# Two RG-LRU tiles moved among the RWKV chunks, their sums moved behind the latents' products, four weight differences on another engine, and a fourth residual buffer

## The chip, the cores and the metric

One core of a Trainium2 chip runs the program. Its engines work from queues of their own and wait for one another by semaphores: TensorE (PE, matmuls; PEld is its loading of the stationary operand), VectorE (DVE), ScalarE (ACT), GpSimd (POOL) and SyncE (SP), which here issues nearly all DMAs. The metric is the device time of one execution in microseconds, lower is better. One execution was also taken by the profiler; its page and its trace are what the text quotes.

## The reference

Two layers of a hybrid block over 512 tokens of width 1024. Each layer norms the residual stream, projects it, feeds three mixers, and adds their gated outputs, projected, to the stream:

```python
for l in range(DEPTH):
    xn = rms_norm(h, ln_g[l])
    proj = xn @ w_in[l]
    u_a, z_a, u_b, z_b, q_lat, kv_lat, k_rope, z_c = jnp.split(proj, pts, axis=-1)
    y_a = rwkv7_mix(u_a, ...)                      # delta rule, 8 heads of 64
    y_b = rms_norm(rglru_mix(u_b, ...), ...)       # gated linear recurrence over 512 channels
    y_c = rms_norm(mla_mix(q_lat, kv_lat, ...))    # latent attention, 8 heads
    y = jnp.concatenate([y_a * silu(z_a), y_b * silu(z_b), y_c * silu(z_c)], axis=-1)
    h = h + y @ w_out[l]
return rms_norm(h, final_g)
```

The second mixer is the one that the change moves:

```python
xc = conv_b + sum(up[:, j:j + T] * conv_w[j] for j in range(4))
gate_r = sigmoid(einsum('bthi,hij->bthj', xb, ga_w) + ga_b)   # gate_i likewise with gx
log_a = -8 * gate_r * softplus(-lam)
a = exp(log_a)
bx = sqrt(-expm1(2 * log_a)) * (gate_i * xc)
h_t = a_t * h_{t-1} + bx_t
```

## The kernel before

All products of a weight with an activation are made of three fp32r matmuls (`mm3`, L231): each operand is split into a high part and the difference to it (low part), and high-high, high-low and low-high are added in PSUM. For weights this is `weights` (L217): SP loads 128x512 into `wr` (three buffers), ACT copies it to `wH`, and POOL or DVE subtracts to make `wL` (four buffers each). Which of the two subtracts is counted: every `wmod`-th call of `weights` goes to DVE, all others to POOL.

A layer is a list of steps, written out as strings (L61 to L63) that `run` goes through. A letter names the step and a digit its tile. `ORD1` is the preparation of the RWKV mixer, `ORD2` its inverses together with gates and projections, `ORD3` the rest:

- `H0` to `H7` (`chunk`, L840) are the eight chunks of 64 tokens of the delta rule. Each needs the state of the one before: matmuls L848, an addition on DVE (L851), matmuls L858, additions on DVE (L862, L863), and every second chunk its output (L876, L882, L884 to L886).
- `A0` to `A3` (`lru_a`, L671) are the four tiles of 128 channels of the RG-LRU: a projection (24 matmuls, two weight loads), the convolution (three L680 on DVE), two gates (L686 on PE, sigmoids on ACT), a product on POOL (L690) and a tanh.
- `B0` and `B1` (`lru_b`, L696) finish tiles 0 and 1, or 2 and 3: exponentials, squares on POOL (L701), L703 and L704 on DVE, square roots, L709 on POOL, the scan (L711), its squares (L717 on ACT) added into `stb` on POOL (L718), and the gating (L719).
- `R0` (`b_sums`, L938) makes the mean square of each token by eight matmuls over `stb` (L378) and a reciprocal root on DVE (`rsb`). `Y0` (`b_split`, L941) splits the four outputs for the product with `w_out`.
- `N0` (`group_norm`, L890) norms the RWKV outputs (small operations L198 to L203 and four L894 on DVE).
- `t0` to `t7` (`lat_products`, L900) are the products of the latents: per step one weight tile of 416 columns (L906) and twelve matmuls, three for each of four token tiles. They use all four `acc` buffers of PSUM. `T0` copies them out, `T1` norms them.
- `g0` to `g3` are the gates 25 to 28 of the attention: a projection into an `acc` buffer, a copy on ACT (L141), a sigmoid, a product on POOL.

Behind `ORD3`, `Q1` (L65) interleaves key, value and query products with `out_parts` (L412, the letter `o`), which adds the RG-LRU's part to the residual stream: for each half of the columns it takes four residual tiles `hp` (L419, tag with three buffers) and four `acc` buffers, multiplies four weight tiles, scales by `rsb` and adds (L427), and writes the tiles to DRAM (L429). `a` steps (`ya_step`, L971) transpose the normed RWKV outputs on PE (L978).

At the start, before the layers, each of four token tiles of `x` is squared on ACT, its reciprocal root is found by small operations on DVE (L245 to L255), it is scaled (L297 on DVE), transposed on PE (L302) and split (L305). The first two projections run among these tiles.

The strings set priorities, not the order itself: when the program is built a planner goes through the instructions of each engine, takes the one with the lowest place in the text among those that its table of costs says are ready, and so fixes the order of every queue. Each engine then runs its queue strictly in that order. So a projection that stands late in the text runs early where PE would otherwise wait, and an instruction whose operands come later than planned holds up all that is queued behind it. The activation function tables (`act`, L133) are used strictly in the order of the text.

Of the kernel before, what the change touches and what calls it, by code (L numbers as in the profile page):

```python
# [12 lines left out]
ALU = mybir.AluOpType  # L13
# [34 lines left out]
def body(ctx, tc, x, wc, wl, wo, w2a2, gagx, wuq, wukv, vec, ln_g, fin_g, cst, out, depth=DEPTH):  # L48
    nc = tc.nc
    V, A, G = nc.vector, nc.scalar, nc.gpsimd  # L50
# [9 lines left out]
    BN = (2, 2, 0, 0)  # L60
    ORD1 = "M0 L0 L1 C0 M1 C1 P0 L2 O0 M2 U1 O1 C2 U2 P1 L3 M3 C3 U0 P2 O2"  # L61
    ORD2 = "G0 U3 G1 P3 G2 Z0 Z1 O3 G3 X0 f4 V0 V1 Z2 Q0 Q1 f0 V2 V3 f1 Q2 Q3 J0 f2 J1 K0 f3 W0 K1 W1 f5 W2 W3"
    ORD3 = "B0 H0 H1 H2 H3 A3 H4 H5 H6 H7 N0 A2 B1 g0 g1 R0 t0 t6 t1 t2 t4 Y0 t5 t3 t7 T0 g2 g3 T1"  # L63
    LO = "0ig12uw3yvcm"
    Q1 = "aoooottttaaaooookvvqvkqvkqkqqqqq"  # L65
    WA, WB, WC, WD = 1000, 2, 2, 5
# [1 line left out]
    def tl(tag, shape, dt=F32, bufs=1):  # L68
        cnt[0] += 1
        return SB.tile(list(shape), dt, tag=tag, name=f"{tag}_{cnt[0]}", bufs=bufs)  # L70
# [4 lines left out]
    def c2(shape=(128, 512), dt=F32):  # L75
        return tl("c2", shape, dt, bufs=7)
# [33 lines left out]
    def acc(shape=(128, 512)):  # L110
        cnt[0] += 1
        return PS.tile(list(shape), F32, tag="acc", name=f"acc_{cnt[0]}", bufs=4)

    def spill():
        cnt[0] += 1
        return DR.tile([128, 512], F32, name=f"dr_{cnt[0]}")
# [23 lines left out]
    def copy(out, in_, **kw):  # L140
        i = A.activation(out=out, in_=in_, func=AF.Copy, **kw)  # L141
        return getattr(i, "ins", i)
# [63 lines left out]
    def f(ap):  # L206
        return ap.bitcast(F32)
# [6 lines left out]
    wn = [0]  # L214
    wmod = [4]

    def weights(src, n=512, raw=None):  # L217

        if raw is None:
            raw = tl("wr", [128, n], F32, bufs=3)  # L220
            nc.sync.dma_start(out=raw, in_=src)
        H = tl("wH", [128, n], F32R, bufs=4)
        L = tl("wL", [128, n], F32R, bufs=4)
        wn[0] += 1
        i = copy(H, raw)
        if behind:
            tc.add_manual_dep(i, behind.pop(0).name, NOSYNC, reason="issue order")
        (V if wn[0] % wmod[0] == 0 else G).tensor_tensor(out=L, in0=raw, in1=f(H), op=ALU.subtract)  # L228
        return H, L

    def mm3(o, a, b, start, stop):  # L231
        PE.matmul(o, a[0], b[0], start=start, stop=False)  # L232
        PE.matmul(o, a[0], b[1], start=False, stop=False)  # L233
        PE.matmul(o, a[1], b[0], start=False, stop=stop)  # L234
# [85 lines left out]
    def one_layer(l):  # L320
# [9 lines left out]
        def proj(j, halves=False):  # L330

            if halves:
                o = acc()
                W = [weights(wc[l, j, :, 4 * hf:4 * hf + 4, :].rearrange("p k c -> p (k c)"), raw=raws.pop((j, hf), None)) for hf in range(2)]
                for th in range(2):
                    t = slice(th * 256, (th + 1) * 256)
                    for k in range(8):
                        s = slice((k % 4) * 128, (k % 4 + 1) * 128)
                        w = W[k // 4]
                        mm3(o[:, t], (w[0][:, s], w[1][:, s]), (xH[:, k, t], xL[:, k, t]), k == 0, k == 7)  # L340
                return o
            o, parts = proj_parts(j)
            for part in parts:
                part()
            return o

        def proj_parts(j):
            o = acc()

            def part(hf):  # L350
                H, L = weights(wc[l, j, :, 4 * hf:4 * hf + 4, :].rearrange("p k c -> p (k c)"))
                for k in range(4):
                    s = slice(k * 128, (k + 1) * 128)
                    kk = 4 * hf + k
                    mm3(o, (H[:, s], L[:, s]), xk(kk), kk == 0, kk == 7)

            return o, [lambda: part(0), lambda: part(1)]
# [33 lines left out]
        def out_steps(m, y):  # L391

            W, os = {}, {}

            def step(n, tt, k):
                if tt == 0 and k == 0:
                    W[n] = [weights(wo[l, m, n, :, i, :]) for i in range(4)]
                if k == 0:
                    os[n, tt] = tl("hp", [128, 512], bufs=3), acc()
                    nc.sync.dma_start(out=os[n, tt][0], in_=hsrc[tt, n])  # L400
                hp, o = os[n, tt]
                c = slice(tt * 128, (tt + 1) * 128)
                mm3(o, (y[k][:, 0, c], y[k][:, 1, c]), W[n][k], k == 0, k == 3)
                if k == 3:
                    V.tensor_tensor(out=hp, in0=o, in1=hp, op=ALU.add)
                    hd = spill()
                    nc.sync.dma_start(out=hd, in_=hp)
                    hsrc[tt, n] = hd

            return [lambda n=n, tt=tt, k=k: step(n, tt, k) for n in range(2) for tt in range(4) for k in range(4)]  # L410

        def out_parts(m, y, rs):  # L412

            os = {}

            def part(n, k):
                if k == 0:
                    for tt in range(4):
                        os[tt] = tl("hp", [128, 512], bufs=3), acc()  # L419
                        nc.sync.dma_start(out=os[tt][0], in_=hsrc[tt, n])  # L420
                W = weights(wo[l, m, n, :, k, :])
                for tt in range(4):
                    c = slice(tt * 128, (tt + 1) * 128)
                    mm3(os[tt][1], (y[k][:, 0, c], y[k][:, 1, c]), W, k == 0, k == 3)
                for tt in range(4) if k == 3 else ():
                    hp, o = os[tt]
                    V.scalar_tensor_tensor(out=hp, in0=o, scalar=rs[:, 2 * tt:2 * tt + 1], in1=hp, op0=ALU.mult, op1=ALU.add)  # L427
                    hd = spill()
                    nc.sync.dma_start(out=hd, in_=hp)  # L429
                    hsrc[tt, n] = hd  # L430

            return [lambda n=n, k=k: part(n, k) for n in range(2) for k in range(4)]
# [212 lines left out]
        def run(order):  # L645
            for s in order.split():
                steps[s[0]](int(s[1]))
# [128 lines left out]
        R0 = {}  # L776
# [169 lines left out]
        run(ORD2)  # L946
        run(ORD3)
        rsb = misc["rsb"]
# [276 lines left out]
```

## Time and profile before

| what | value |
|---|---|
| time, median of 3 runs | 868.64 us (867.18 to 869.16) |
| the profiled execution: time, span | 868.69 us, 866.8 us |
| mean granted TensorE clock | 0.978 |
| RWKV chunks (first L858 to the latents' products) | 204.4 to 255.1 us and 627.8 to 678.3 us |
| latents' products (to gate 27) | 255.1 to 284.6 us and 678.3 to 707.7 us |
| bytes over DMA | 91.08 MB, mean 105 GB/s |

The first of each pair is layer 0, the second layer 1. In rows of the trace the columns are the start, the time taken, engine, line and operation, output and input, the number of instructions merged in the row, and in brackets the idle time before it with what ended it. In rows of waits they are who waited, for whom, total, times, longest. In windows they are the length, the busy time of each engine with the number of instructions, the granted clock (1.00 is full speed), the share of the DMA engines and GB/s. In groups they are line, engine, operation, shapes and count, then busy time and mean ns of one, then the idle time before them.

### The profile page before, as it was taken

The page shows a single profiled execution, that of the slowest core. Times are in us where ns is not written, and L with a number is a line of the kernel's source. Part 1 is how long each engine was busy: PE and PEld are TensorE (multiplying, and loading weights), DVE is VectorE, ACT ScalarE, POOL GpSimd, SP SyncE. Part 2 cuts the span into 40 slices and gives each one's busy share as a digit, 9 for nine tenths or more (in the row PEclk, how much of TensorE's full clock was granted, in tenths as well). Part 3 has the DMA queues.
Part 4 walks back from the last instruction along what each step waited for, and adds up shares of the span by engine and source line. Part 5 has one row for each costly group of instructions (what it writes and reads, how often), then busy time and mean ns, then how long its engine had stood idle before and what let it go on. Part 6 is the DMA issues. An engine that isn't in the chain of part 4 may idle for free.

```text
span 866.8 us, 15212 instructions
## 1 busy us (share of the span) xinstructions
PE 801.0 (92%) x5696; PEld 624.3 (72%) x5696; DVE 574.6 (66%) x1169; ACT 506.2 (58%) x990; POOL 332.3 (38%) x303
## 2 busy tenths in 40 slices
PE   3999999999896999999989999999998699999995
PEld 2877888877676867566778788888766597765674
DVE  5678776924887485875474866694367856777736
ACT  5667875656544635574367677745572644455635
POOL 2355557513325431011444556574151544210123
PEclk9999999999998989999999999999999989999998
DMA  6322233310112465122743233232101134741354
GB/s 218 115 70 69 72 110 134 116 51 26 31 43 81 136 206 186 56 87 96 250 139 98 74 98 106 89 109 92 39 14 51 45 107 137 232 130 50 109 170 159
DMA packets 49755, 91.08 MB, mean 105 GB/s; under 512 B 5520, under 2 KB 8336, under 8 KB 49680
## 3 DMA queue, kind: packets, MB, share of 16 engines
q1 hardware_dynamic: 49104, 89.05, 31.8%
q8 instruction: 45, 0.74, 0.3%
q10 hardware_dynamic: 576, 1.05, 0.3%
q14 instruction: 30, 0.25, 0.1%
HBM read 73.30 MB, written 16.78 MB: 104 GB/s over the span
## 4 chain that ended last, share of the span: by engine, by line
PE 43%; DVE 10%; ACT 5%; DMA 3%; issue 2%; POOL 2%; SPq 0%; ACTq 0%; DVEq 0%; POOLq 0%
PE acc L232 9%; PE acc L233 9%; PE acc L234 9%; PE acc L1057 4%; PE ck L1083 3%; PE ps L1075 2%; DMA hp<-dr 1%; ACT g L138 1%; DMA wr<-in_wo_dram 1%; ACT UV L141 1%; DVE c L460 1%; PE ps L686 1%; PE ps L610 1%; ACT wH L141 1%; DVE wL L228 1%
## 5 line engine op out<-in xcount | busy, mean ns | idle before, releaser
L228 POOL TENSOR_TENSOR wL<-wr,wH 128x512 fp32r<-128x512 f32 (+1 forms) x130 | 175.6, 1355 | 308.7 <-ACT wH L141 301.8
L141 ACT ACTIVATE wH<-wr 128x512 fp32r<-128x512 f32 (+1 forms) x192 | 119.0, 622 | 139.7 <-PE acc L233 73.3
L232 PE MATMUL acc<-xH,wH 128*128 128x512 f32 (+1 forms) x496 | 191.4, 387 | 0.0
L233 PE MATMUL acc<-xL,wH 128*128 128x512 f32 (+1 forms) x496 | 189.8, 383 | 0.4 <-DVE xL L305 0.3
L234 PE MATMUL acc<-xH,wL 128*128 128x512 f32 (+1 forms) x496 | 189.4, 382 | 0.0
L232 PEld LDWEIGHTS acc<-xH,wH 128*128 128x128 f32 x496 | 94.0, 190 | 19.2 <-issue 1.6
L233 PEld LDWEIGHTS acc<-xL,wH 128*128 128x128 f32 x496 | 94.3, 190 | 17.6 <-DVE xL L305 1.2
L234 PEld LDWEIGHTS acc<-xH,wL 128*128 128x128 f32 x496 | 94.2, 190 | 17.1
L228 DVE TENSOR_TENSOR wL<-wr,wH 128x512 fp32r<-128x512 f32 (+1 forms) x62 | 47.3, 765 | 69.0 <-ACT wH L141 68.4
L232 PE MATMUL acc<-wH,c 128*128 128x512 f32 x192 | 83.7, 436 | 2.5 <-DVE hp L427 1.2
L233 PE MATMUL acc<-wL,c 128*128 128x512 f32 x192 | 77.6, 404 | 1.1 <-DVE wL L228 1.1
L234 PE MATMUL acc<-wH,c 128*128 128x512 f32 x192 | 77.3, 403 | 0.0
L141 ACT ACTIVATE UV<-ps 64x512 f32<-64x512 f32 (+4 forms) x112 | 52.4, 494 | 32.0 <-PE ps L1075 22.5
L232 PEld LDWEIGHTS acc<-wH,c 128*128 128x128 f32 x192 | 37.2, 194 | 12.8 <-ACT c L141 2.9
L138 ACT ACTIVATE c<-acc,sm 128x128 f32<-128x128 f32 (+3 forms) x64 | 33.5, 526 | 19.4 <-DVE sm L1059 19.1
L233 PEld LDWEIGHTS acc<-wL,c 128*128 128x128 f32 x192 | 37.1, 193 | 9.5 <-DVE wL L228 1.5
L1057 PE MATMUL acc<-am,am 128*128 128x128 f32 (+3 forms) x128 | 42.3, 447 | 0.9 <-ACT c L138 0.8
L234 PEld LDWEIGHTS acc<-wH,c 128*128 128x128 f32 x192 | 36.9, 192 | 8.6 <-issue 0.5
L138 ACT ACTIVATE g<-g 128x512 f32<-128x512 f32 (+1 forms) x58 | 36.1, 626 | 8.4 <-DVE g L704 6.5
L136 ACT ACT_TABLE_LOAD x31 | 39.8, 1283 | 1.3 <-PEq L1213 0.7
L141 ACT ACTIVATE c<-g 128x512 fp32r<-128x512 f32 (+1 forms) x40 | 25.0, 630 | 21.5 <-DVE g L980 16.1
L368 POOL TENSOR_TENSOR g<-g,g 128x512 f32<-128x512 f32 x24 | 32.6, 1360 | 10.4 <-ACT g L138 10.4
(221 smaller groups left out, 1604.4 us busy)
## 6 DMA issues: line engine op xcount, KB each, us to landing
wr<-in_wc_dram SPq DMA_DIRECT2D x116, 256.0 KB, 2.7
wr<-in_wo_dram SPq DMA_DIRECT2D x48, 256.0 KB, 3.4
hp<-dr SPq DMA_DIRECT2D x40, 256.0 KB, 3.2
dr<-hp SPq DMA_DIRECT2D x32, 256.0 KB, 2.8
dr<-g SPq DMA_DIRECT2D x16, 256.0 KB, 2.6
g<-dr SPq DMA_DIRECT2D x16, 256.0 KB, 2.9
wr<-in_wl_dram SPq DMA_DIRECT2D x16, 208.0 KB, 2.5
c<-in_x_dram SPq DMA_DIRECT2D x8, 256.0 KB, 6.5
```

Source lines behind the costliest of these rows:

```text
L136: chained(A.preload_act_table_set(SETS[st]))
L138: chained(A.activation(out=out, in_=in_, func=func, **kw))
L141: i = A.activation(out=out, in_=in_, func=AF.Copy, **kw)
L228: (V if wn[0] % wmod[0] == 0 else G).tensor_tensor(out=L, in0=raw, in1=f(H), op=ALU.subtract)
L232: PE.matmul(o, a[0], b[0], start=start, stop=False)
L233: PE.matmul(o, a[0], b[1], start=False, stop=False)
L234: PE.matmul(o, a[1], b[0], start=False, stop=stop)
L368: G.tensor_tensor(out=z, in0=z, in1=s, op=ALU.mult)
L460: V.scalar_tensor_tensor(out=hv, in0=o, scalar=rs[:, 2 * tt:2 * tt + 1], in1=hp, op0=ALU.mult, op1=ALU.add)
L1057: PE.matmul(o[:, 0:n], qT[:, hd, qt * 128:n], K2[:, p, e, 0:n], start=True, stop=True)
L1075: PE.transpose(o[:, (qt - kt) * 128:(qt - kt + 1) * 128], Pm[p][e, qt][:, kt * 128:(kt + 1) * 128], ident)
L1083: i = PE.matmul(ot[e * 64:(e + 1) * 64, k2 * 128:T], Vt[:, k2, 2 * p + e, :], PT[:, 2 * (k2 % 2) + e, 0:(4 - k2) * 128], start=(k2 == 0), ...
```

## The change

```diff
-    ORD3 = "B0 H0 H1 H2 H3 A3 H4 H5 H6 H7 N0 A2 B1 g0 g1 R0 t0 t6 t1 t2 t4 Y0 t5 t3 t7 T0 g2 g3 T1"
+    ORD3 = "B0 H0 H1 A2 H2 H3 A3 H4 H5 H6 H7 B1 N0 g0 g1 t0 t6 t1 t2 t4 t5 t3 t7 T0 R0 Y0 g2 g3 T1"
...
-        (V if wn[0] % wmod[0] == 0 else G).tensor_tensor(out=L, in0=raw, in1=f(H), op=ALU.subtract)
+
+        (V if wn[0] % wmod[0] == 0 or wn[0] <= 4 else G).tensor_tensor(out=L, in0=raw, in1=f(H), op=ALU.subtract)
...
-                        os[tt] = tl("hp", [128, 512], bufs=3), acc()
+                        os[tt] = (tl("hp", [128, 512], bufs=3) if tt < 3 else c2()), acc()
```

`A2` goes from behind the group norm to behind the second chunk. `B1` goes ahead of the group norm. `R0` and `Y0` go behind the latents' products and their copies. The first four calls of `weights` in the program (the projections 12 and 0 of layer 0) subtract on DVE. In `out_parts` the fourth residual tile of each half comes from the pool `c2` (seven buffers, L76), which the chunks' outputs and later the attention's probabilities also use. No operation is added or left out.

## The prediction

> **What bounds the kernel now.** First the page's head and busy table, then the waits of PE stage by stage, then the stretch with the largest wait in windows and in order of time. Both layers show it alike; the rows are layer 1's where none is named.
>
> ```profile
> span 866.8 us, 15212 instructions
> PE 801.0 (92%) x5696; PEld 624.3 (72%) x5696; DVE 574.6 (66%) x1169; ACT 506.2 (58%) x990; POOL 332.3 (38%) x303
> ...
> 255.12:284.56 29.44, 22.77 (x110) 21.54 (x109) 22.09 (x35) 15.23 (x25) 16.51 (x12) 0.88 0.22 68
> 678.27:707.74 29.47, 22.81 (x110) 21.58 (x108) 22.17 (x35) 15.20 (x25) 16.54 (x12) 0.88 0.22 69
> ...
> PE ck L378 <- POOL sqn L718: 5.2, 1, 5.2
> PE acc L233 <- DVE wL L228: 1.5, 1, 1.5
> ```
>
> PE is busy for 801.0 of 866.8 us, so 65.8 us of it are idle, and what ends late on PE sets the time. The two windows run from the first product of the latents to the first of gate 27, in layer 0 and in layer 1 (columns: length, then PE, PEld, DVE, ACT, POOL busy, the granted clock, DMA). PE stands idle for 29.47 - 22.81 = 6.66 us of each, in two waits: 5.2 us of the token sums (L378) for POOL, 1.5 us of a product for a weight difference from DVE.
>
> ```profile
> 678.27 0.35 PE L232 MATMUL acc<-wH,xH 128*128 128x416 f32 x1
> 679.95 0.35 PE L232 MATMUL acc<-wH,xH 128*128 128x416 f32 x1
> 686.82 0.35 PE L234 MATMUL acc<-wH,xL 128*128 128x416 f32 x1
> 678.77 4.19 DVE L894 TENSOR_TENSOR c<-c,vr 128x512 f32<-128x512 f32 x4
> 682.88 1.28 DVE L703 SCALAR_TENSOR_TENSOR g<-g,g 128x512 f32<-128x512 f32 x2
> 685.30 2.53 POOL L709 TENSOR_TENSOR g<-g,g 128x512 f32<-128x512 f32 x2 [3.50 <-ACT g L138]
> 689.65 3.11 POOL L718 TENSOR_TENSOR sqn<-sqn,g 128x512 f32<-128x512 f32 x2 [1.82 <-ACT g L717]
> 691.11 0.58 ACT L141 ACTIVATE g<-acc 128x512 f32<-128x512 f32 x1
> 692.81 1.86 PE L378 MATMUL ck<-ones,sqn 128*128 128x2 f32 x8 [5.21 <-POOL sqn L718]
> 692.00:694.00 2.00, 1.19 (x6) 1.19 (x6) 1.31 (x1) 0.81 (x2) 2.00 (x2) 0.50 0.00 0
> 696.00:698.00 2.00, 2.00 (x7) 1.90 (x7) 1.93 (x5) 1.55 (x3) 1.08 (x1) 0.50 0.00 0
> 698.00:700.00 2.00, 2.00 (x11) 1.96 (x10) 1.90 (x6) 0.55 (x1) 1.33 (x1) 0.87 0.42 107
> ```
>
> The rows in order of time show why. Step B1 (L699 to L720 for tiles 2 and 3) stands behind the group norm: its L703 starts at 682.88, when L894 has let DVE go. Then follow square root, L709, scan, square and L718, one engine waiting for the next, and L378 stands in PE's queue ahead of the remaining products. A second cause hides under it. From 678.27 to 686.82 PE runs 36 products: four weight tiles for three token tiles each (4 x 3 x 3). The fourth token tile needs the accumulator of gate 26, which ACT copies out only at 691.11, behind the squares of B1. So it is not enough to move the sums: B1 must be early as well. After the wait the granted clock is 0.50 from 692.81 to 698 (the first and the last of three windows stand here) and 0.87 to 700, which loses half of 5.19 us and 0.13 of 2, or 2.9 us. The stall's whole price is **6.66 + 2.9 = 9.6 us a layer**.
>
> **The change, part by part.** *Sums behind the products, B1 ahead of the group norm.* R0 now comes after T0. Its eight matmuls and the vector work on `rsb` remain; the first use is L427, behind 48 matmuls of gates 27 and 28 and 48 of the first output half, 18 us even at the 0.187 us below, so R0 is hidden. Behind L378 on PE now stand gate 27's products, and they would wait only if B1 were late by the whole run of the latents' products. Y0 issues the same splits later, with the same cover. What is late next is the products' supply: from the first to the tenth start is 1.68 us, 0.187 each, so a tile of 12 asks for its weights every 2.24 us. The 1.5 us wait for DVE came behind L894, L703 and L704; with B1 gone, L894 is still there. I keep 1.0 us of it (bounds 0 and 1.5). The stage gives **8.6 us a layer**.
>
> *A2 among the chunks.* Nothing is added: the same 24 matmuls, two weight loads, three L680, gates and activations, ahead of H2 instead of behind N0. The planner already fills the gaps between chunk steps with the projections of A3, A2 and gates 25 and 26, so on PE and in SP's queue A2 and A3 only change places. What moves is behind the projection: A2's three L680 now outrank H2, A3's gates come before H4, and B1 with its two table changes and six POOL operations falls into H4 to H7, where DVE's queue also holds the additions L851, L862 and L863 that the next chunk's matmuls wait for.
>
> ```profile
> 627.80:655.90 28.10, 25.11 (x345) 18.16 (x344) 19.64 (x36) 16.21 (x26) 11.60 (x10) 1.00 0.13 39
> 655.90:674.30 18.40, 17.64 (x279) 12.60 (x278) 11.74 (x25) 6.47 (x13) 3.13 (x3) 1.00 0.09 25
> L680 DVE SCALAR_TENSOR_TENSOR g<-g,vecs,g 128x512 f32<-128x512 f32 x4 | 3.0, 746 | 0.0
> L719 DVE SCALAR_TENSOR_TENSOR g<-g,vecs,g 128x512 f32<-128x512 f32 x2 | 2.5, 1262 | 0.0
> L711 DVE TENSOR_TENSOR_SCAN g<-g,g 128x512 f32<-128x512 f32 x2 | 2.4, 1224 | 0.6 <-POOL g L709 0.6
> L703 DVE SCALAR_TENSOR_TENSOR g<-g,g 128x512 f32<-128x512 f32 x2 | 1.4, 692 | 1.8 <-POOL g L701 0.9 <-POOL g L675 0.9
> L709 POOL TENSOR_TENSOR g<-g,g 128x512 f32<-128x512 f32 x2 | 2.6, 1280 | 4.2 <-ACT g L138 4.2
> L863 DVE TENSOR_TENSOR S<-S,PC x12: 404/416/428, 218.3 to 669.8; 128x256 f32<-128x256 f32 x12
> ```
>
> The first window is B0 and the early chunks, the second the late ones. B0 is the same work for tiles 0 and 1, and beside it PE idles 28.10 - 25.11 = 3.0 us; without it 18.40 - 17.64 = 0.8. If B1 does to the late chunks what B0 does to the early ones, that is 2.2 us a layer. B1's DVE part is 2.5 + 2.4 + 1.4 and some 0.8 for L704, about 7.1 us, and DVE is free for 18.40 - 11.74 = 6.7 us of that window, plus the 3.0 us of four L680 that leave it; projections still stand ready. Bounds are a gain of 0.8, the idle that there is to lose, and all of it in the chunks' chain: 7.1 us and six L680 of 0.75, or 11.6. I take **1.5 us** a layer, near the row of B0, and the remaining products as cover; without that cover it is the 2.2.
>
> *First four differences on DVE.*
>
> ```profile
> 11.88 0.16 DVE L254 SCALAR_TENSOR_TENSOR sm<-sm,sm 128x1 f32<-128x1 f32 x1
> 12.50 2.49 POOL L228 TENSOR_TENSOR wL<-wr,wH 128x512 fp32r<-128x512 f32 x2 [11.04 <-ACT wH L141]
> 12.55 1.23 DVE L255 SCALAR_TENSOR_TENSOR sm<-sm,sm 128x1 f32<-128x1 f32 x1
> 13.82 2.38 DVE L297 SCALAR_TENSOR_TENSOR g<-c,sm,c 128x512 f32<-128x512 f32 x2
> 18.99 1.26 DVE L253 TENSOR_TENSOR sm<-sm 128x1 f32<-128x1 f32 x1
> 20.29 1.20 DVE L254 SCALAR_TENSOR_TENSOR sm<-sm,sm 128x1 f32<-128x1 f32 x1
> 21.71 1.41 DVE L297 SCALAR_TENSOR_TENSOR g<-c,sm,c 128x512 f32<-128x512 f32 x2
> 22.61 0.63 PE L302 MATMUL ps<-C,g 128*128 128x128 f32 x4 [1.79 <-DVE g L297]
> 31.98 0.68 DVE L228 TENSOR_TENSOR wL<-wr,wH 128x512 fp32r<-128x512 f32 x1
> ```
>
> Beside POOL's pairs a one-column operation takes 1.23, 1.26 and 1.20 us instead of 0.16, and a pair of L297 2.38 instead of 1.41: 1.07 + 1.10 + 1.04 + 0.97 = 4.2 us on the chain that PE's transposes (L302) wait for. That leaves; four differences of 0.68 us come to the same queue, 2.7 us if all stand ahead of the chain, nothing if they fall between. So 1.5 to 4.2 us; I take **2.5**, since later only 1.79 us of PE idle are left to close besides the first 2 us.
>
> *Fourth residual buffer.*
>
> ```profile
> 755.62 0.32 SPq L420 DMA_DIRECT2D hp<-dr  x1
> 760.98 0.75 DVE L427 SCALAR_TENSOR_TENSOR hp<-acc,sm,hp 128x512 f32<-128x512 f32 x1 [5.08 <-DMA hp<-dr]
> 761.78 0.50 PE L232 MATMUL acc<-c,wH 128*128 128x512 f32 x1 [1.17 <-DVE hp L427]
> ```
>
> The fourth load is issued at 755.62, when a buffer is written out; L427 waits for it and PE for L427, 1.17 us in layer 1. With its own buffer the load is early, and SP's queue loses a waiting issue. In layer 0 no PE wait has this cause: **1.2 us** in all (bounds 0 and 2.4, the same in both layers). The buffer comes from a pool of seven of which the chunks' four outputs hold four, so nothing else waits for it.
>
> **The sum** against the profiled execution, 868.69 us (span 866.8 and 1.9 around it; the median of the runs is 868.64): 2 x (8.6 - 1.5) + 2.5 + 1.2 = 17.9, so 850.8 us; its own range is 846 to 856.
>
> **The rivals.**
>
> *The stall is only shortened.*
>
> ```profile
> 733.45 0.77 PE L232 MATMUL acc<-wH,c 128*128 128x512 f32 x1 [1.24 <-DVE hp L427]
> 734.00:736.00 2.00, 2.00 (x6) 1.60 (x5) 2.00 (x4) 0.97 (x2) 0.54 (x1) 0.50 0.93 315
> ```
>
> The clock is at 0.50 here behind a wait of 1.24 us, so short waits can cost the clock too. If 1.5 us remain in each layer, for a difference on DVE or for gate 26's accumulator, and the clock drops for as long as now (2.9), the stage gives 9.6 - 4.4 = 5.2: 868.69 - 2 x 3.7 - 3.7 = 857.6. For it: L894 still holds DVE for 4.19 us. Against: three weight tiles are split ahead. The Trainium skill, "TensorE: Matmul & The Clock Gate", Part 1, halves the clock only after an idle window of about 3.4 us; by that the 1.5 us would cost nothing more, and the time would be 851.8 us. The row above speaks against it.
>
> *POOL holds up the chunk chain.* L863 has both inputs in SBUF, and no L863 of the trace meets a POOL operation (404 to 428 ns throughout). At the start such operations stood for a whole POOL one. If L863 of the last three chunk steps waits 1.28 us each (L709's mean), 3.8 us replace the 1.5: 855.4. The Trainium skill, "SBUF — State Buffer", Who interferes with whom, says that a VectorE instruction with two SBUF inputs and a GpSimd one that reads SBUF exclude each other; the start's rows agree.
>
> *All of it falls away*: no wait in the products, chunks free, start 4.2: 868.69 - 19.2 - 4.2 - 1.2 = 844.1.
>
> *Slower.* The 11.6 us of outranking vector work all land between two chunks' matmuls while PE has no projection left: 2 x (11.6 - 8.6) - 3.7 gives 871.0. It decides once the chunks lose 10.5 us a layer. Against: 6.7 us of DVE are free there.
>
> *The order does not follow the text*: the planner leaves L378 in the products; only start and buffer count, 865.0.
>
> **How the numbers follow.** Forecast 0.50, shortened 0.16, POOL 0.12, all 0.11, slower 0.06, order 0.05. A measurement of this kernel tells about 0.2%, or 1.7 us, from no change. The order case may end on either side of 867.0 and I halve it: faster 0.91, same 0.03, slower 0.06. The range, 843 to 860, takes in the first four cases, less the ends of the chunks' bounds.
>
> **What would show it.** The products' window at 20 to 22 us with a clock of 1.00, and no wait of L378 for POOL; L711's second pair before L894; idle in the late chunks' window below 2.5 us; L255 at 0.16 at the start; no wait of L427 for its load at 761. A products' window still above 25 us, or chunks more than 4 us longer, would make the prediction wrong.

## The result, and the profile after

The changed kernel takes 860.22 us (median of four runs, 855.86 to 861.77); the kernel before takes 868.9 beside it. The ratio is 0.9893, 95% interval 0.9852 to 0.9934. The forecast of 850.8 us had the direction right and the size wrong: 1.07% were won, 2.1% were forecast. The median lies at the upper end of the range, 860, and 0.2 us above it. Rows of the changed kernel have line numbers one higher than before from L229 on (L378 is now L379, L427 is L428, L711 is L712, L863 is L864).

The profiled execution took 855.86 us, 12.8 us less than the one before. The same marks on PE cut both spans into the same stretches:

| stretch, us | before, layers 0 and 1 | after | won | forecast |
|---|---|---|---|---|
| start to the first product of the layer (layer 0 alone) | 66.4 | 63.2 | 3.2 | 2.5 |
| chunks, to the first product of the latents | 50.7, 50.4 | 58.1, 58.1 | -15.0 | -3.0 |
| products of the latents | 29.3, 29.3 | 17.9, 18.8 | 21.8 | 17.2 |
| from there to the attention's first product with `qT` (gates, out_parts, norms) | 62.2, 61.9 | 60.7, 60.6 | 2.9 | 1.2 |
| all | | | 12.9 | 17.9 |

Three terms came in larger than forecast and one, the chunks, took back 15.0 us where 3.0 were set down. The windows of the changed kernel's chunks and products (length, PE, PEld, DVE, ACT, POOL busy, granted clock, DMA share, GB/s):

```profile
201.29:259.35 58.06, 49.01 (x640) 35.65 (x639) 44.10 (x70) 34.53 (x54) 26.28 (x21) 0.94 0.18 53
259.35:277.29 17.94, 17.94 (x97) 17.90 (x95) 11.11 (x22) 6.97 (x14) 5.86 (x5) 0.99 0.32 96
...
619.61:677.69 58.08, 48.20 (x639) 34.90 (x639) 44.10 (x70) 34.41 (x54) 26.28 (x21) 0.96 0.16 48
677.69:696.46 18.77, 18.77 (x96) 18.59 (x95) 10.23 (x22) 6.96 (x14) 6.21 (x5) 0.95 0.30 93
```

and the kernel before in layer 1, for the two stretches whose windows were not shown, the chunks and what lies behind the products:

```profile
627.84:678.27 50.43, 46.67 (x639) 33.37 (x639) 34.97 (x71) 26.11 (x43) 16.85 (x14) 1.00 0.12 35
...
707.55:769.43 61.88, 56.90 (x246) 45.41 (x245) 38.73 (x86) 30.53 (x62) 18.85 (x15) 0.94 0.58 181
```

The products are now wholly busy: 17.94 of 17.94 and 18.77 of 18.77 us. In the chunks of layer 1 PE does the same 639 matmuls, but is idle for 58.08 - 48.20 = 9.9 us instead of 50.43 - 46.67 = 3.8, and the same work takes 1.5 us more because the clock is 0.96 instead of 1.00. The largest waits of PE over the whole span say for whom:

```profile
PE ck L849 <- DVE S L864: 9.2, 6, 3.1
PE ps L883 <- DVE UV L852: 5.3, 7, 1.6
PE ps L687 <- DVE g L681: 4.2, 2, 2.1
```

Before, in layer 1's chunks, L848 waited 2.1 us for the state (L863), L882 1.6 for the chunk's sums (L851), and A2's gates (L686) not at all. Half of each of these rows is a layer's, on average: 4.6, 2.7 and 2.1 us. The longest wait, 3.1 us, is the one ahead of the last chunk. In order of time, first PE, then DVE, then POOL:

```profile
665.60 0.69 PE L859 MATMUL ck<-UV,c 128*64 128x64 f32 x16
...
671.67 0.51 PE L849 MATMUL ck<-S,c 64*64 64x64 f32 x10 [3.12 <-DVE S L864]
...
656.19 0.42 DVE L864 TENSOR_TENSOR S<-S,PC 128x256 f32<-128x256 f32 x1
...
665.27 3.42 DVE L712 TENSOR_TENSOR_SCAN g<-g,g 128x512 f32<-128x512 f32 x2
668.73 0.42 DVE L863 TENSOR_TENSOR S<-ck,S 128x256 f32<-128x256 f32 x1
669.07 1.14 DVE L229 TENSOR_TENSOR wL<-wr,wH 128x416 fp32r<-128x416 f32 x1
670.14 1.48 DVE L864 TENSOR_TENSOR S<-S,PC 128x256 f32<-128x256 f32 x1
...
667.58 3.75 POOL L719 TENSOR_TENSOR sqn<-sqn,g 128x512 f32<-128x512 f32 x2
```

The sums of the chunk are in PSUM when L859 ends, at 665.60 + 0.69 = 666.29. L863, which adds them to the state, starts at 668.73, because B1's two scans stand ahead of it in DVE's queue: 2.4 us. A weight difference then takes 1.14 us, and L864, which multiplies the sum by the decay `PC` and so makes the new state, 1.48 us instead of 0.42, both beside POOL's additions L719. The gates of A2 (L687, at 642.41 behind a wait of 2.10 us) are another case. Their three convolutions L681 stand in DVE's queue among B0's scan and gating:

```profile
635.46 1.40 DVE L681 SCALAR_TENSOR_TENSOR g<-g,vecs,g 128x512 f32<-128x512 f32 x1
636.79 1.21 DVE L712 TENSOR_TENSOR_SCAN g<-g,g 128x512 f32<-128x512 f32 x1
637.92 0.72 DVE L681 SCALAR_TENSOR_TENSOR g<-g,vecs,g 128x512 f32<-128x512 f32 x1
...
639.16 1.43 DVE L720 SCALAR_TENSOR_TENSOR g<-g,vecs,g 128x512 f32<-128x512 f32 x1
640.51 1.75 DVE L681 SCALAR_TENSOR_TENSOR g<-g,vecs,g 128x512 f32<-128x512 f32 x1
```

Behind the wait for the state PE pays a second time, here from 674 on:

```profile
674.00:680.00 6.00, 5.66 (x41) 5.18 (x42) 4.39 (x11) 3.14 (x7) 0.45 (x1) 0.53 0.25 80
```

The granted clock is 0.53 over six microseconds behind the wait.

### The profile page after: what moved, and what is told of

The parts are those of the page before. It is cut to its first block, busy times and chain, and to the rows that moved or that the text cites. A ratio compares the mean times of both kernels' runs of the same rounds, so it can differ in the third digit from the quotient of the medians.

```text
span 854.0 us, 15206 instructions
## 1 busy us (share of the span) xinstructions
PE 796.6 (93%) x5696; PEld 621.0 (73%) x5696; DVE 571.6 (67%) x1173; ACT 506.2 (59%) x990; POOL 325.7 (38%) x299
## 4 chain that ended last, share of the span: by engine, by line
PE 69%; DVE 16%; ACT 8%; issue 3%; DMA 2%; POOL 1%; SPq 1%; ACTq 0%; DVEq 0%; POOLq 0%
PE acc L233 16%; PE acc L234 16%; PE acc L235 15%; PE acc L1058 4%; PE ck L1084 3%; ACT g L138 2%; PE ps L1076 2%; PE ps L687 1%; DVE g L681 1%; PE ps L611 1%; ACT UV L141 1%; ACT L136 1%; DVE wL L229 1%; PE ps L629 1%; PE ps L786 1%
## 5 line engine op out<-in xcount | busy, mean ns | idle before, releaser
L229 POOL TENSOR_TENSOR wL<-wr,wH 128x512 fp32r<-128x512 f32 (+1 forms) x126 | 169.7, 1350 | 290.0 <-ACT wH L141 266.0
L141 ACT ACTIVATE wH<-wr 128x512 fp32r<-128x512 f32 (+1 forms) x192 | 118.8, 622 | 140.6 <-PE acc L234 74.5
L229 DVE TENSOR_TENSOR wL<-wr,wH 128x512 fp32r<-128x512 f32 (+1 forms) x66 | 49.9, 760 | 72.8 <-ACT wH L141 72.7
L141 ACT ACTIVATE UV<-ps 64x512 f32<-64x512 f32 (+4 forms) x112 | 52.4, 494 | 30.9 <-PE ps L1076 22.6
L233 PEld LDWEIGHTS acc<-wH,c 128*128 128x128 f32 x192 | 36.7, 191 | 12.8 <-ACT c L141 3.0
L141 ACT ACTIVATE c<-g 128x512 fp32r<-128x512 f32 (+1 forms) x40 | 24.9, 630 | 34.3 <-DVE g L981 22.4
L138 ACT ACTIVATE c<-acc,sm 128x128 f32<-128x128 f32 (+3 forms) x64 | 33.6, 528 | 19.1 <-DVE sm L1060 18.8
```

Source lines behind the costliest of these rows:

```text
L138: chained(A.activation(out=out, in_=in_, func=func, **kw))
L229: (V if wn[0] % wmod[0] == 0 or wn[0] <= 4 else G).tensor_tensor(out=L, in0=raw, in1=f(H), op=ALU.subtract)
```

## The experiments

The theory after the result: the order wins the stall whole and loses most of it to three waits in the chunks, which B1's scans, POOL's operations beside them and A2's early gates make. Its rivals: the other two edits disturb the chunks; A2's place alone does it; POOL alone does it.

### The three edits one by one

*The order alone*: the kernel before with only the ORD3 of the change.

> The kernel before with the new order string alone. Theory: the order wins about 11 us a layer in the latents' products and pays 7.5 of them back in the chunks, 2 x 3.5 = 7 us, so about 862 us, with the same three waits in the chunks as the changed kernel (gates of A2 for the convolutions, L849 for the state, L883 for a chunk's sums), together 9 to 10 us of idle from the first chunk to the last. Rival 1: the chunks' loss comes from the other two edits, through the planner; then the order alone keeps what was forecast, 2 x 7.1 = 14 us, about 855 us, and the chunks idle 4 to 5 us. Rival 2: the order wins nothing by itself (chunks take it all), 868 to 870 us.

It took 867.14 us, ratio 0.9969 (0.9949 to 0.9989).

```profile
PE ck L848 <- DVE S L863: 4.6, 3, 3.1
PE ps L882 <- DVE UV L851: 2.3, 4, 1.6
PE ps L686 <- DVE g L680: 2.1, 1, 2.1
```

These rows of its waits in layer 1's chunks are those of the changed kernel, and its stretches are too (chunks 58.1 and 58.1, products 18.5 and 18.3 us). So the loss in the chunks belongs to the order, and the first rival falls. Without the fourth buffer the stretch behind the products is 62.5 us in both layers: there the gain of the whole change isn't the order's. The order is worth 0.3%, where 14.2 us, 1.6%, were forecast for it. It is also less than the theory's 7 us; its profiled execution, at 863.15, is among the fastest of its twelve runs (862.79 to 871.42).

*The first four differences alone*:

```diff
-        (V if wn[0] % wmod[0] == 0 else G).tensor_tensor(...)
+        (V if wn[0] % wmod[0] == 0 or wn[0] <= 4 else G).tensor_tensor(...)
```

> The kernel before with the first four differences on DVE alone. Theory: the stretch from the first PE instruction to the first product is 2.5 to 3 us shorter, the rest is the same: about 866 us, and L255 at the start takes 0.16 us instead of 1.23. Rival: the start is shorter and the time is lost again before the first chunk: 868.5 to 869 us.

It took 865.93 us, ratio 0.9970 (0.9955 to 0.9986): 2.6 us, where 2.5 were forecast. The changed kernel's DVE rows at the start show why:

```profile
12.15 0.15 DVE L256 SCALAR_TENSOR_TENSOR sm<-sm,sm 128x1 f32<-128x1 f32 x1
12.22 0.68 DVE L229 TENSOR_TENSOR wL<-wr,wH 128x512 fp32r<-128x512 f32 x1
12.82 1.41 DVE L298 SCALAR_TENSOR_TENSOR g<-c,sm,c 128x512 f32<-128x512 f32 x2
```

With no POOL operation beside them the one-column operations take 0.16 us, not 1.23, and the pair of L298 1.41, not 2.38. The differences are not free: three of the four stand between steps of the same chain (at 12.22, and at 17.10 and 17.77 between the one-column operations of the next tile) and hold it up by 0.6 us each. So 4.2 - 3 x 0.6 = 2.4 us are left of the forecast's 4.2, near the 2.66 us by which the stretch to the first product is shorter in this run (63.71 us instead of 66.37).

*The fourth residual buffer alone*:

```diff
-                        os[tt] = tl("hp", [128, 512], bufs=3), acc()
+                        os[tt] = (tl("hp", [128, 512], bufs=3) if tt < 3 else c2()), acc()
```

> The kernel before with the fourth residual buffer alone. Theory: it wins what was forecast in one layer, 1.2 us, and up to the 2.9 us by which the two stretches from the latents' products to the first score are shorter after the change: 866 to 867.7 us. Rival: those stretches are shorter because of the order (no waiting sums in front of the output's products), and the buffer by itself wins nothing: 868.9 us.

It took 863.86 us, ratio 0.9946 (0.9924 to 0.9967): 4.7 us, the largest of the three, where 1.2 were forecast with 2.4 as the upper bound. The additions into the residual tiles on DVE in layer 1, before, with the load of the first half's fourth tile:

```profile
732.56 1.40 DVE L427 SCALAR_TENSOR_TENSOR hp<-acc,sm,hp 128x512 f32<-128x512 f32 x2
...
734.48 0.74 DVE L427 SCALAR_TENSOR_TENSOR hp<-acc,sm,hp 128x512 f32<-128x512 f32 x1
736.03 0.32 SPq L420 DMA_DIRECT2D hp<-dr  x1
...
741.47 0.74 DVE L427 SCALAR_TENSOR_TENSOR hp<-acc,sm,hp 128x512 f32<-128x512 f32 x1
...
750.64 2.05 DVE L427 SCALAR_TENSOR_TENSOR hp<-acc,sm,hp 128x512 f32<-128x512 f32 x3
...
760.98 0.75 DVE L427 SCALAR_TENSOR_TENSOR hp<-acc,sm,hp 128x512 f32<-128x512 f32 x1 [5.08 <-DMA hp<-dr]
```

and with the buffer alone:

```profile
730.45 1.40 DVE L427 SCALAR_TENSOR_TENSOR hp<-acc,sm,hp 128x512 f32<-128x512 f32 x2
...
732.37 0.74 DVE L427 SCALAR_TENSOR_TENSOR hp<-acc,sm,hp 128x512 f32<-128x512 f32 x1
733.03 0.73 DVE L427 SCALAR_TENSOR_TENSOR c<-acc,sm,c 128x512 f32<-128x512 f32 x1
...
745.75 1.39 DVE L427 SCALAR_TENSOR_TENSOR hp<-acc,sm,hp 128x512 f32<-128x512 f32 x2
...
747.67 0.73 DVE L427 SCALAR_TENSOR_TENSOR hp<-acc,sm,hp 128x512 f32<-128x512 f32 x1
748.33 0.73 DVE L427 SCALAR_TENSOR_TENSOR c<-acc,sm,c 128x512 f32<-128x512 f32 x1
```

In both halves the fourth addition was late: 7.0 us behind the third in the first half, 10.3 behind the first three in the second. For the first half the trace names no wait before it, since other work stands between in DVE's queue. But SP's rows show the load itself late: it was issued only at 736.03, when a first buffer had been written out, and the quickest of these loads took 3.2 us to land, so the addition could not run before some 739. With the buffer alone both fourth loads are issued at 667.6 and 668.1, ahead of the products of the latents. Now all four of a half come within 3.3 us. The prediction looked only at the one wait that the trace named, at 761, and not at the whole half. The stretch behind the products is shorter, in layer 1:

```profile
705.42:763.34 57.92, 54.64 (x246) 43.22 (x246) 38.50 (x86) 30.39 (x62) 18.54 (x15) 1.00 0.57 185
```

It fell from 62.2 and 61.9 to 59.0 and 57.9 us in the profiled executions; of these 7.2 us 2.5 are idle of PE (4.0 and 5.0 us before, 3.2 and 3.3 with the buffer) and the rest is clock (0.92 and 0.94 before, 0.97 and 1.00). How much of the clock's part is owed to the buffer these two executions can't tell: see the last section.

By their ratios the three edits won 2.7, 2.6 and 4.7 us, 10.0 together. The whole change won 9.3 us, and 10.7 in its second set of runs (below), so within the noise the three add up.

### Must A2 and B1 move at all?

*Sums and splits alone*:

```diff
-    ORD3 = "B0 H0 H1 H2 H3 A3 H4 H5 H6 H7 N0 A2 B1 g0 g1 R0 t0 t6 t1 t2 t4 Y0 t5 t3 t7 T0 g2 g3 T1"
+    ORD3 = "B0 H0 H1 H2 H3 A3 H4 H5 H6 H7 N0 A2 B1 g0 g1 t0 t6 t1 t2 t4 t5 t3 t7 T0 R0 Y0 g2 g3 T1"
```

> The kernel before with only the token sums and the splits moved behind the latents' products; A2 and B1 stay behind the group norm. Theory: the products then wait for the accumulator of gate 26, which ACT copies behind B1's squares at 691; about 1.7 us a layer are won, the chunks stay as they were (50.5 us from the first chunk to the first product): 865 to 866 us, and an idle of 4 us or more is left in the products. Rival: moving the sums is enough; the products lose the whole 9.6 us a layer and the chunks lose nothing, 849 to 852 us, and the moves of A2 and B1 were only a cost.

It took 868.82 us, ratio 0.9995 (0.9978 to 1.0012): nothing. The longest wait in layer 1's products:

```profile
PE ck L378 <- POOL sqn L718: 5.2, 1, 5.2
```

The stall is as long as before (6.7 us of idle in each layer). The sums stand later in the text, yet on PE they run at the same place, at 695.85 with products still to come: the fourth token tile has no accumulator before B1's squares are done, which would explain why the planner takes the sums first. Even the 1.7 us of the theory were too much. The prediction's remark that the sums alone are not enough holds, for that reason.

*B1 behind the group norm again*, the rest as changed (`... H6 H7 N0 B1 g0 ...`).

> The changed kernel with B1 behind the group norm instead of ahead of it. PE's own order is the same; DVE, ACT and POOL change. Theory: the waits of L849 for the state and of L883 for the chunk's sums go back to 2.1 and 1.6 us, about 3.9 us a layer and some half clock are won in the chunks, the wait of A2's gates (2.1 us) stays, and the products wait again for the accumulator of gate 26, 4 us or more: within 3 us of the changed kernel's 860, 857 to 863. Rival: the waits in the chunks come from A2 alone, and B1 only gives back the stall: 865 us or more.

It took 859.19 us, ratio 0.9878 (0.9861 to 0.9896), as the changed kernel. The time is inside what the theory named, but its reason fell: the waits did not go back.

```profile
PE ck L849 <- DVE S L864: 4.6, 3, 3.1
PE ps L883 <- DVE UV L852: 2.4, 4, 1.6
PE ps L687 <- DVE g L681: 2.1, 1, 2.1
```

B1's operands are there while the norm still waits for the last chunk, so B1 runs among the chunks whichever of the two stands first. What brings B1 there is A2's place: with A2 behind the norm, in the sums alone, layer 1's chunks kept their 50.4 us.

*A2 behind H3, A3 behind H5*:

```diff
-    ORD3 = "B0 H0 H1 A2 H2 H3 A3 H4 H5 H6 H7 B1 N0 ...
+    ORD3 = "B0 H0 H1 H2 H3 A2 H4 H5 A3 H6 H7 B1 N0 ...
```

> The changed kernel with A2 behind H3 and A3 behind H5, so further back among the chunks. Theory: A2's gates wait 2.1 us for the convolutions because DVE is still at work on B0 then; later they don't: 2 us a layer less, 853 to 855 us against the 858 to 860 of the changed kernel; the waits for B1's work, 4.6 and 3.0 us in a layer, stay. Rival: the gates wait wherever they stand, or B1, pushed later, now holds up the last chunk and the products as well: 858 us or more, with the idle from the first chunk to the first product still 9 us or more.

It took 856.03 us, ratio 0.9851 (0.9827 to 0.9875).

```profile
620.43:672.32 51.89, 46.53 (x640) 33.84 (x639) 35.97 (x66) 30.96 (x50) 20.50 (x17) 1.00 0.12 36
672.32:696.58 24.26, 20.64 (x96) 20.00 (x95) 18.50 (x27) 10.24 (x18) 12.59 (x10) 0.86 0.35 110
```

The chunks are back at 51.9 us, but 3.6 us of idle and the half clock return to the products: PE waits 3.62 us at 677.97 for ACT's copy of an accumulator (L141), which stands behind the squares of the second scan. Half of each forecast came. The wait of A2's gates is gone, as the theory had it, and B1 now holds up the products, as the rival had it. But the chunks' idle is 5.4 us, where the rival asked for 9 or more, and the 856.03 us lie between the two; the interval overlaps with that of the changed kernel's second set (0.9857 to 0.9897), so only the stretches tell them apart. The loss goes where B1 goes.

*A2 behind the chunks, B1 behind the gates*: `... A3 H4 H5 H6 H7 A2 g0 g1 B1 N0 t0 ...`.

> A new order: A2 behind the chunks as in the kernel before, then gates 25 and 26, then B1 and the group norm, the sums behind the products; the two other edits stay. Theory: B1 needs only to be behind the gates, so that gate 26's accumulator is copied out early, and not among the chunks: the chunks take 51 us again, the products keep most of their gain: 2 x 3.5 to 2 x 7 us less than the changed kernel, 846 to 853 us. Rival: what bounds the products is DVE, which then has L894, B1 and the weight differences at once: 3 us or more of waiting for a difference in each layer, 858 us or more.

It took 855.27 us, ratio 0.9837 (0.9810 to 0.9864): 5 us better than the changed kernel's first median, 2.6 than its second (below), and short of the theory's 853; against the second set the intervals overlap. In layer 1 the chunks take 50.4 us and the products 21.4, with 2.8 of idle in waits for weight splits; right behind them the sums wait 1.6 us for POOL, and that stretch grows to 64.1 and 62.3 us. So the chunks can be spared, and the work then costs behind them.

### What makes the state late?

*The changed kernel once more*:

> The changed kernel once more, with nothing altered. Theory: its runs lie apart by their mean granted clock (0.979 to 0.984 in those seen, 0.005 of 860 being 4.3 us), so a further set has a median within 2 us of 860 and a spread of 4 us or more, and the profile shows the same waits in the chunks (9 to 10 us of idle). Rival: the profiled 855.86 us was the kernel's own time and the slower runs were disturbed: the median falls to 856 to 857.

857.85 us (857.22 to 861.64), ratio 0.9877 (0.9857 to 0.9897), with 9.1 us of idle in the chunks of each layer. The waits are the same to 0.1 us; the clock isn't (0.92 over layer 1's chunks here, 0.96 in the first profile).

*The scans held behind the last update of the state*, by an order on DVE alone, without a semaphore:

```diff
-                V.tensor_tensor_scan(out=hs, data0=a, data1=bx, initial=0.0, ...)
+                i = V.tensor_tensor_scan(out=hs, data0=a, data1=bx, initial=0.0, ...)
+                if j >= 2:
+                    tc.add_manual_dep(i, <last L864>, NOSYNC, reason="issue order")
```

> The changed kernel with B1's two scans (L712) held behind the last update of the state (L864) on DVE; nothing else is asked for. Theory: the 3.12 us wait of L849 in each layer is the scans' 2.4 us and the slow L864 (1.48 us beside POOL's sum, 0.42 without) ahead of the chain; it falls to about 0.6, and 2.5 us of wait and the half clock behind it go: 3 to 4 us a layer, 853 to 855 us. Rival: the chain is late for another reason (the sums L852 behind L704), and the wait moves one chunk on: 860 us.

It took 848.95 us (848.28 to 850.5), ratio 0.9767 (0.9751 to 0.9782): 8.9 us less than the changed kernel beside it, more than the theory gave. DVE in layer 1, where L866 and L867 are the addition and the multiplication of the state, L713 the scans:

```profile
662.99 0.42 DVE L866 TENSOR_TENSOR S<-ck,S 128x256 f32<-128x256 f32 x1 [0.23 <-PE ck L862]
663.45 0.74 DVE L867 TENSOR_TENSOR S<-S,PC 128x256 f32<-128x256 f32 x1
664.11 2.33 DVE L713 TENSOR_TENSOR_SCAN g<-g,g 128x512 f32<-128x512 f32 x2
```

and the windows of the chunks and products of layer 1 (layer 0 has 53.32 and 18.58 us, both at 1.00):

```profile
616.26:669.59 53.33, 46.49 (x639) 33.52 (x639) 40.25 (x66) 33.29 (x51) 24.43 (x21) 1.00 0.18 53
669.59:688.30 18.71, 18.15 (x97) 17.70 (x95) 13.93 (x27) 7.94 (x16) 7.59 (x6) 1.00 0.25 77
```

DVE now waits for PE (0.23 us) and not PE for DVE. The 3.12 us wait is gone, the clock is 1.00 in both stretches, and the chunks take 4.7 us less in each layer. The products keep their gain. The constraint also makes the planner reorder some matmuls of the inverses, but the stretch from there to the chunks stays at 138.1 us in both layers. This version is faster than both kernels.

*Both, scans held and A2 behind H3*:

> Both at once: the scans held behind the last update of the state, and A2 behind H3. Theory: the two waits are independent, so the 2.1 us of A2's gates go from the 6.8 us of idle that the held scans left: 849 - 4 = 845 us. Rival: A2 later brings B1 so late that its products or sums are waited for in the products of the latents: 849 us or more.

857.14 us, ratio 0.9856 (0.9838 to 0.9873). The rival held: the two moves don't add. The chunks take 51.9 and 53.4 us, but the products 24.4 and 21.8, idle for 3.7 and 3.2 us in waits for an accumulator and for weight differences, behind B1.

*POOL's additions with the token sums*: L719 for tiles 2 and 3 moved in the text into `b_sums`.

> The changed kernel with POOL's two additions of B1 (L719, the squares of tiles 2 and 3 into sqn) issued with the token sums, behind the products, instead of among the chunks; the scans stay where they are. It tells POOL's share of the late state from the scans' own. Theory: the scans stand ahead of L863 on DVE's queue and are the larger part; without POOL beside them the second scan and L864 get back to 1.22 and 0.42 us, 1 to 2 us of the 3.1 us wait: 855 to 857 us, against 849 for the held scans. Rival: POOL is the whole cause, the wait of L849 goes to 0.6 us or less and the half clock with it: 849 to 851 us.

859.44 us, ratio 0.9873 (0.9853 to 0.9894). It told nothing apart: the planner issued the two additions as early as before, at 670.65, beside the scans. So the next kernel forbids it.

*POOL's additions held behind the state*, with the scans left ahead of it:

```diff
-                    G.tensor_tensor(out=stb[0], in0=stb[0], in1=sq, op=ALU.add)
+                    i = G.tensor_tensor(out=stb[0], in0=stb[0], in1=sq, op=ALU.add)
+                    if j >= 2:
+                        tc.add_manual_dep(i, <last L864>, SYNC, reason="behind the state")
```

> The changed kernel with POOL's two additions of B1 (L719) made to wait for the last update of the state (L864), while the two scans stay ahead of that update on DVE. It tells POOL's share of the late state from the scans' place. If the place in DVE's queue is the cause: L863 still starts behind the scans, 2.4 us after its matmuls; only what POOL slows is won, some 0.7 us of L864 (1.48 down to the 0.74 of the held scans) and up to 1 us of the scan (3.42 the pair, 2.33 with POOL quiet); the wait before the last chunk goes from 3.1 to 1.5 to 2.5 us, 854 to 858 us. If POOL is the cause: the wait goes below 1 us and the clock stays at 1.00 behind it, 849 to 852 us, as with the held scans. If neither: 3.1 us and 858 to 860 us.

853.5 us, ratio 0.9813 (0.9798 to 0.9828); the matmuls of the inverses are reordered here as with the held scans. DVE in layer 1, with the line numbers of the kernel with held scans:

```profile
666.79 3.43 DVE L713 TENSOR_TENSOR_SCAN g<-g,g 128x512 f32<-128x512 f32 x2
670.26 0.42 DVE L866 TENSOR_TENSOR S<-ck,S 128x256 f32<-128x256 f32 x1
670.60 0.58 DVE L229 TENSOR_TENSOR wL<-wr,wH 128x416 fp32r<-128x416 f32 x1
671.10 0.42 DVE L867 TENSOR_TENSOR S<-S,PC 128x256 f32<-128x256 f32 x1
```

The wait ahead of the last chunk falls from 3.12 to 1.47 us. L864's counterpart is back at 0.42 us, the difference at 0.58; the scans still take 3.43, so it isn't L719 that slows them. The additions of POOL are 1.06 + 0.56 = 1.6 us of the 3.1, and the scans' place the remaining 1.5. Of that 1.5, too, 1.1 may be POOL's: the pair of scans took 2.33 us in the kernel with held scans, where POOL was idle beside them, and 3.43 here, where POOL works on a weight difference (667.68 to 669.14). No run has the scans ahead of the state with POOL quiet.

With the two medians of the changed kernel (857.85, 860.22) POOL's additions cost 4.4 to 6.7 us, and the scans' place another 853.5 - 848.95 = 4.6 us. By the chunks of the two layers in the profiled executions (58.1 and 58.1 us, here 56.4 and 56.3, with held scans 53.3 and 53.3) it is 3.4 and 6.1 us. Both causes are there; which of them is the larger, these runs leave open.

## Why the prediction was right in direction and wrong in size

- *The stall of the products.* The whole price of 9.6 us a layer was right, and it left whole: no wait of L379 for POOL, windows of 17.9 and 18.8 us where 20 to 22 were named. The 1.0 us kept for a weight difference did not come. The term of 8.6 measured 10.5 to 11.3, but part of this only moved: the eight matmuls of the sums (1.86 us at half clock) and four transposes (L978, 0.60 us) ran inside the stretch before, and the stretch behind it now has 259 matmuls instead of 246.
- *The start.* 2.5 us forecast, 2.6 measured alone: the 4.2 us went, and 1.8 us of differences came into the chain, within the bounds named.
- *The fourth buffer.* 1.2 us forecast, bounds 0 and 2.4; 4.7 measured alone. "In layer 0 no PE wait has this cause" is true of PE's waits (there DVE waits 3.36 us for the same load, at 337.90, and PE is busy); but what the buffer changed in the first half shows as a late load and an order, not as a wait. The rows to read were the issues of the loads and the times of the four additions of each half.
- *The chunks: the term that failed.* Forecast **1.5 us a layer**, "near the row of B0, and the remaining products as cover"; measured 7.4 and 7.65, inside the bound of 11.6, and beyond the sign that the prediction itself gave for being wrong, chunks more than 4 us longer; the one wait of 3.12 us is also more than the 2.5 us of idle that it allowed the late chunks. In layer 1 the idle went from 3.8 to 9.9 us and the work slowed by 1.5. The row of B0 measures how much vector work the early chunks bear, but not where it stands: two scans ahead of L863, on the one chain that the next chunk needs, held it up by 2.4 us, POOL's additions lengthened what followed, and PE's products ran out (at 668.55) before the chain came through. The 6.7 us of free DVE time in that window were no help, since a queue in order can't put an addition that becomes ready during a scan ahead of it. The half clock behind the wait was priced for the products and left out here. And the 2.1 us of A2's gates was no term at all: the text said that A2's three convolutions outrank H2, but not that A2's own gates would wait for them behind B0's work.
- *The rivals.* POOL holding up the chunk chain was 855.4, from 3.8 us in place of the 1.5; the additions held give 853.5, so the mechanism is real, with 4.4 to 6.7 us by the medians where the rival had 2 x 3.8. It falls on the last two updates, L864 with 1.11 us (at 661.78, beside L710) and 1.48 (beside L719) instead of 0.42, and on a weight difference, where the rival added 1.28 to each of three. The Trainium skill, "SBUF — State Buffer", Who interferes with whom, calls the port that VectorE and GpSimd share an exclusive lock; the 1.48 us of L864 beside L719 and 0.42 without agree. The stall was not shortened but gone, so that rival falls; the slower one needed 10.5 us a layer lost in the chunks, though it was right that PE's products run out; that the order doesn't follow the text is what the sums alone showed (868.82), not the change.

The sum again: 17.9 forecast, less 12.0 in the chunks, plus 4.6 in the products, 1.7 behind them and 0.7 at the start gives the 12.9 us of the profiled execution. So that the time came as near as it did is in part luck: 7.0 us that the other terms won beyond their forecast covered more than half of the 12.0. That execution is the fastest of its four; the others were 3.6 to 5.9 us slower, with granted clocks of 0.982 to 0.979 against its 0.984.

## What to carry to other kernels

Work that is moved beside a serial chain is to be priced by what it stands in front of in an in-order queue, not by how much of it the queue has room for; and the half clock behind each new wait belongs into the price. Where a planner fixes the order, a step moved in the text may run where it ran before, and what a missing buffer costs may show as a late load and a changed order, without a wait: look at when the instructions run. One ordering constraint that keeps two long vector operations off the chain was worth about as much as the whole change.

## What the runs showed of the hardware

The same idle of PE cost the half clock in one execution and not in another. Ahead of 734 us in the kernel before, two gaps of 0.62 and 1.24 us lie within 2.5 us; with the buffer alone there are two of 0.62 and 1.23 at the same instructions. The windows behind them, the kernel before and then the buffer alone:

```profile
734.00:740.00 6.00, 6.00 (x21) 4.67 (x20) 4.06 (x6) 1.95 (x4) 1.30 (x1) 0.54 0.80 253
```

```profile
731.80:737.80 6.00, 5.81 (x34) 4.35 (x33) 5.47 (x10) 3.45 (x6) 2.60 (x2) 1.00 0.98 332
```

The clock is 0.54 in one and 1.00 in the other, which is 2.8 us of such a stretch. The Trainium skill, "TensorE: Matmul & The Clock Gate", Part 1, has the gate watch a free-running window of about 3.4 us, which would make the outcome depend on where a gap falls; but it asks for an idle window, and here the 1.9 us of idle that the trace names were enough. No run here settles it. It may bear on the spread: runs of the changed kernel lie 5.9 us apart, those with the scans held, whose clock is 1.00 through chunks and products, 2.2 us. What was left untried is a kernel with shifted phase and otherwise equal order.
